# Half-projection pacing of tile 0's weight scalings, output-weight stores a step later, and the last pair's sums and output products woven in

## The chip, the cores and the metric

One core of one Trainium2 chip runs the whole program as a single launch. The metric is device microseconds from start to end; the time before is the median of three runs, 2706.23 us (2701.7 to 2709.22). A core has five engines that run side by side, each through its own list of instructions in order: TensorE (PE, matmuls and transposes), VectorE (DVE), ScalarE (ACT), GpSimd (POOL) and SyncE (SP, which here issues every DMA). They wait for each other through semaphores alone.

## The reference, cut to what matters

A trunk of two layers over 2048 frames of 1024 channels in float32: a gated MLP mixer, then attention in chunks of 64 frames, where each chunk sees itself and the 8 chunks before it. The change touches the second layer only.

```python
def chunk_attention_mixer(h, k_pad, v_pad, w_qz, rel_bias, w_out):
    q, z = jnp.split(h @ w_qz, 2, axis=-1)
    ...
        sc = jnp.einsum('bqhd,bkhd->bhqk', qc, kc).astype(jnp.float32) + bias
        sc = jnp.where(valid[None, None, None, :], sc, NEG_INF)
        p = jax.nn.softmax(sc, axis=-1).astype(vc.dtype)
        return jnp.einsum('bhqk,bkhd->bqhd', p, vc)
    ...
    return (o * jax.nn.silu(z)) @ w_out

    h = rms_norm(x, b_norm_g[i])
    x = x + chunk_attention_mixer(h, k_pad, v_pad, ...)
    return rms_norm(x, final_norm_g)
```

K and V come once from the residual stream behind the first layer, normalised with their own gain.

## The kernel before

**Numbers.** Every float32 factor is split in two: a part rounded for TensorE (`wh`, `hi`, `Sho`; a cast on ACT) and what is left (`wl`, `lo`, `Slo`; a subtraction on DVE). `mm3` (L113 to L115) multiplies with three matmuls: high by high, high by low, low by high.

**Stages.** The first layer takes about half of the time and then V follows for all tiles. From about 1530 us the attention runs over 4 tiles `t` of 512 frames, and in each over 8 pairs `p` of heads: tile 0 to about 1730, tile 1 to 2050, tile 2 to 2330, tile 3 to 2649 us. A pair has 8 steps `u` (two heads, four blocks of 128 queries). A step scores a block two steps ahead (`s`, L1324), takes its row maximum on DVE and its exp on ACT, scales it by the sum on POOL (`pr`, L1343), and transposes a block (`flip`: `tp`, L1359), which is then cast to `pt` on ACT and completed on DVE (L1363, L1364). There is one PSUM buffer for `tp`, so the next transpose waits for DVE's part of the last. At the step's end of each head `pv` (L1384) multiplies `pt` with V; `ot` (ACT), `og` (DVE) and a gate close it.

**What fills TensorE between the steps.** A generator (`ahead`, L1593) yields single groups of matmuls, and the main loop (L1627) takes an even share at each half step. In it are the projections of the next pair (`one`, L1234: 8 groups of three for each of Q, K and the gate), and the output product of the tile before (`outs[t - 1]`). That product is a Strassen scheme (`strassen`, L260): 7 products `PHS` of 2 halves with 12 matmuls each, named `bo_<product>_<half>`, in 4 generator steps. Its right sides are weights (`wh_bo`, `wl_bo`) from DRAM, which live in 8 buffers, enough for two products; its left sides are sums of attention outputs, split into `Sho` and `Slo`.

**The weights of the projections.** For each pair and each of three matrices `weights` (L213) loads 128 x 1024 numbers. In tile 0 POOL multiplies them by the norm's gain (`scaled`, L194) and they are stored to `wk`; ACT casts (L209) and DVE subtracts (L210). Later tiles load the scaled ones from `wk` (L218).

**The weights of the output product** are summed once, by `o_sums` (L298), during the first four pairs of tile 1: four blocks `wo` are loaded (L306), POOL forms sums, and each of seven products is cast (`so_<product>h`, L313), completed (`so_..l`) and stored (`ows`, L316; one in `owf`, L311). The `so` tiles share four buffers.

**The last pair.** Behind tile 3 no attention is left, so its own output product runs alone. `last_open` (L1449) loads tile 3's attention outputs of pairs 0 to 5 ahead of the last pair and forms the left sums (`s3`, then `s1`, `s2`, `s4`, all on POOL; written as A_hl from A_hh and A_hl in the profile). Pairs 6 and 7 are written into the left sides by DVE (`last_og`, L1474), with the rest of the sums behind each. During the last pair `ahead` gives 12 steps of tile 2's product; the whole of `outs[3]` comes behind it.

**What sets the order.** Tile's list scheduler puts each engine's instructions in order at build time. Two helpers bend it with dependencies that exist for the scheduler alone and make no semaphore: `on_beat` (L174) ties an instruction behind the last transposes of the step, `paced_by_pj` (L183) behind the latest entry of `pace`, which `one` appends to at the first group of each projection (L1241).

Of the kernel before, what the change touches and what calls it, by code (L numbers as in the profile page):

```python
# [22 lines left out]
NT = S // T  # L23
# [10 lines left out]
def trunk_kernel(  # L34
# [148 lines left out]
    def paced_by_pj(ins):  # L183
        if pace:
            tc.add_manual_dep(
                ins.ins, pace[-1],
                mybir.DependencyInfo(mybir.DependencyClass.NoSync, mybir.DependencyReason.DATA),
                reason="order",
            )
# [23 lines left out]
    def weights(t, p, c):  # L213
        name = f"b{t}_{p}_{c}"
        raw = raw_w(t, f"raw_{name}")
        w = w_tile(f"wh_{name}"), w_tile(f"wl_{name}")
        if t:
            nc.sync.dma_start(raw[:], wk3[p][c][:])  # L218
        else:
            nc.sync.dma_start(raw[:], w_kqz[p, :, c, :])  # L220
            paced_by_pj(scaled(raw, (bg if c else kg)[:, :, :]))
            nc.sync.dma_start(wk3[p][c][:], raw[:])
        hi = split_in(raw, *w)
        if t:
            paced_by_pj(hi)
        return w
# [72 lines left out]
    def o_sums(u, place, s_place):  # L299
# [8 lines left out]

        def keep(ph, src):
            if ph == 5:  # L310
                nc.sync.dma_start(owf[q][:, cs], src)  # L311
# [3 lines left out]
            for n, y_ in enumerate((hi, lo)):  # L315
                nc.sync.dma_start(ows[ph, q][:, n, cs], y_[:].bitcast(F32))  # L316
# [17 lines left out]
        ]  # L334
# [876 lines left out]
    with ExitStack() as bctx:  # L1211
# [22 lines left out]
        def one(t, p, c):  # L1234
            wh, wl = weights(t, p, c)
            acc = pmm.tile([P, T], F32, tag="mm", name=f"pj{t}_{p}_{c}")
            for k in range(KD):
# [3 lines left out]
                if k == 0:  # L1241
                    pace.append(ins.ins.name)
# [206 lines left out]
        def last_open():  # L1449
# [9 lines left out]
            for cs in (slice(0, 512), slice(512, 1024)):  # L1459
                tg(la["s3"][:, cs], la["00"][:, cs], la["10"][:, cs], op=sub)  # L1460
            last_sums(slice(0, 512))

        def last_sums(cs):
            x_ = {n: a[:, cs] for n, a in la.items()}
            tg(x_["s1"], x_["10"], x_["11"], op=add)
            tg(x_["s2"], x_["11"], x_["s3"], op=sub)
            tg(x_["s4"], x_["01"], x_["s2"], op=sub)

        def last_og(p, og32, z):
# [7 lines left out]
            last_sums(slice(k * 256, k * 256 + 256))  # L1477
# [120 lines left out]
        def ahead(t, p):  # L1598
# [8 lines left out]
            else:  # L1607
# [6 lines left out]
                if t:  # L1614
                    yield from some(outs[t - 1], 8)

        def steps_of(t, p):
            n = (32 if p == 0 else 24) if p + 1 < NPAIR else (16 if t + 1 < NT else 0)
            return n + SHARE[t][p]
# [10 lines left out]
        for t in range(NT):  # L1630
            for p in range(NPAIR):
                gen = ahead(t, p) if t + p else first
                total = steps_of(t, p) - (0 if t + p else 8)
                if t + 1 == NT and p + 1 == NPAIR:
                    last_open()
                per = 11 if p + 1 == NPAIR and t + 1 < NT else 16
                todo = []
                if t == 1 and p < 4:
# [89 lines left out]
```

## Time and profile before

| what | value |
|---|---|
| runs | 2701.7, 2706.23, 2709.22 us; median 2706.23 |
| profiled execution | 2705.63 us, of which the span is 2703.8 us |
| mean granted clock of TensorE | 0.992 |
| PE busy | 2625.2 us in 12960 records |
| DVE, ACT, POOL busy | 1887.0, 1295.5, 887.1 us |
| DMA | 735.53 MB, mean 272 GB/s |

The span is the stretch from the first to the last instruction of one profiled execution; the rest of that execution's time lies around it. Rows of the timeline give the start in us from the span's begin, the duration in us, engine, line, operation, what is written from what, and the count; in brackets stands how long the engine was idle before and what ended that. A row of the windows gives a stretch, its length, the busy time of PE, PEld (weight loads), DVE, ACT and POOL with counts, the granted clock, the DMA share and GB/s. A matmul's row overlaps the next, since PE is pipelined: the distance of two starts tells its cost.

### The profile page before, as it was taken

The numbers are of one execution on the slowest core, as the hardware profiler recorded it, in microseconds if no ns is written. First come the engines' busy times: TensorE is split into PE (matmuls) and PEld (weight loads), VectorE is DVE, ScalarE is ACT, GpSimd is POOL, SyncE is SP. The second block draws the span as 40 slices with busy tenths as digits, with TensorE's granted clock in tenths as the row PEclk, the third lists the DMA queues.
The fourth block names the chain that finished last, engine by engine and source line by source line (L and its number), as shares of the span: only waits on it lengthen the run. The fifth ranks groups of instructions, "written<-read, shape, count | busy, mean of one in ns | idle before, by whom it ended". The sixth has DMA issues, their size and how long they took to land.

```text
span 2703.8 us, 38109 instructions
## 1 busy us (share of the span) xinstructions
PE 2625.2 (97%) x12960; PEld 2188.7 (81%) x12960; DVE 1887.0 (70%) x2937; ACT 1295.5 (48%) x2296; POOL 887.1 (33%) x874
## 2 busy tenths in 40 slices
PE   8999999999999999999989999999998999999997
PEld 7888888888888888888868777777887888888875
DVE  5655676666677668757677766788767667866676
ACT  5422242443434435333365456666555555655553
POOL 3511335142251414115043344333332223313243
PEclk9999999999999999999999999999999999999999
DMA  7898999989988879858666677788889667766567
GB/s 297 313 328 329 343 363 324 333 318 342 329 314 280 309 257 333 294 203 274 247 241 210 221 250 228 223 275 293 281 264 292 203 217 241 254 204 197 183 228 245
DMA packets 274771, 735.53 MB, mean 272 GB/s; under 512 B 29585, under 2 KB 61329, under 8 KB 274577
## 3 DMA queue, kind: packets, MB, share of 16 engines
q1 hardware_dynamic: 274576, 733.09, 78.5%
q8 instruction: 104, 1.70, 0.3%
q14 instruction: 91, 0.74, 0.1%
HBM read 540.56 MB, written 181.93 MB: 267 GB/s over the span
## 4 chain that ended last, share of the span: by engine, by line
PE 77%; DVE 8%; DMA 7%; issue 3%; POOL 2%; ACT 2%; SPq 1%; DVEq 0%; POOLq 0%; ACTq 0%
PE P L115 11%; PE P L114 11%; PE P L113 11%; PE pj L113 5%; PE pj L115 5%; PE pj L114 5%; PE pv L1384 4%; PE s L1324 4%; PE tp L1359 3%; PE Po L115 2%; PE Po L113 2%; PE Po L114 2%; PE vp L115 2%; PE vp L114 2%; PE vp L113 2%
## 5 line engine op out<-in xcount | busy, mean ns | idle before, releaser
L113 PE MATMUL P<-T,S 128*128 128x512 f32 x1248 | 496.0, 397 | 2.1 <-ACT S L386 2.1
L115 PE MATMUL P<-T,S 128*128 128x512 f32 x1248 | 490.3, 393 | 0.0
L114 PE MATMUL P<-T,S 128*128 128x512 f32 x1248 | 489.1, 392 | 1.1 <-DVE T L389 1.1
L1343 POOL TENSOR_SCALAR pr<-pr,sl 128x640 f32<-128x640 f32 (+4 forms) x256 | 196.3, 768 | 543.3 <-DVE sl L1342 486.8
L113 PE MATMUL pj<-hh_b,wh_b 128*128 128x512 f32 x768 | 319.6, 416 | 1.8 <-ACT hh_b L168 1.0
L115 PE MATMUL pj<-hh_b,wl_b 128*128 128x512 f32 x768 | 304.7, 397 | 0.3 <-DVE wl_b L210 0.2
L114 PE MATMUL pj<-hl_b,wh_b 128*128 128x512 f32 x768 | 303.3, 395 | 0.0
L1339 ACT ACTIVATE pr<-pr,nm 128x640 f32<-128x640 f32 (+4 forms) x256 | 195.4, 763 | 192.8 <-DVE nm L1332 184.7
L115 PEld LDWEIGHTS P<-T,S 128*128 128x128 f32 x1248 | 235.3, 189 | 50.3
L113 PEld LDWEIGHTS P<-T,S 128*128 128x128 f32 x1248 | 235.9, 189 | 47.4 <-ACT S L386 2.3
L114 PEld LDWEIGHTS P<-T,S 128*128 128x128 f32 x1248 | 235.7, 189 | 46.9 <-DVE T L389 1.3
L1364 DVE TENSOR_TENSOR pt<-tp,pt 128x640 fp32r<-128x640 f32 (+4 forms) x256 | 188.8, 738 | 55.4 <-ACT pt L1363 52.1
L1332 DVE CUSTOM_DVE_ANT_0 pr<-s,bias 128x640 f32<-128x640 f32 (+4 forms) x256 | 188.1, 735 | 30.5 <-PE s L1324 26.2
L1363 ACT CAST pt<-tp 128x640 fp32r<-128x640 f32 (+4 forms) x256 | 159.1, 622 | 61.4 <-PE tp L1359 57.6
L1359 PE MATMUL tp<-ident,pr 128*128 128x128 f32 x1120 | 168.4, 276 | 19.0 <-DVE pt L1364 13.1
L1359 PEld LDWEIGHTS tp<-ident,pr 128*128 128x128 f32 x1120 | 130.8, 141 | 54.9 <-issue 22.3
L115 PEld LDWEIGHTS pj<-hh_b,wl_b 128*128 128x128 f32 x768 | 144.9, 189 | 32.9 <-DVE wl_b L210 1.7
L1384 PEld LDWEIGHTS pv<-pt,V 128*128 128x128 f32 x896 | 144.3, 191 | 31.5 <-DVE pt L1364 11.6
L1384 PE MATMUL pv<-pt,V 128*128 128x256 f32 (+3 forms) x896 | 158.5, 323 | 9.2 <-DVE pt L1364 6.4
L113 PEld LDWEIGHTS pj<-hh_b,wh_b 128*128 128x128 f32 x768 | 145.9, 190 | 19.9 <-ACT wh_b L209 1.6
L114 PEld LDWEIGHTS pj<-hl_b,wh_b 128*128 128x128 f32 x768 | 145.9, 190 | 17.5 <-issue 0.2
L210 DVE TENSOR_TENSOR wl_b<-raw_b,wh_b 128x1024 fp32r<-128x1024 f32 x96 | 126.9, 1322 | 42.3 <-ACT wh_b L209 41.0
(284 smaller groups left out, 5715.6 us busy)
## 6 DMA issues: line engine op xcount, KB each, us to landing
S<-hsd SPq DMA_DIRECT2D x288, 512.0 KB, 5.4
rw<-in_w_a SPq DMA_DIRECT2D x108, 512.0 KB, 6.3
A<-ytd SPq DMA_DIRECT2D x72, 512.0 KB, 5.7
raw_b<-wk SPq DMA_DIRECT2D x72, 512.0 KB, 4.7
hsd<-S SPq DMA_DIRECT2D x56, 512.0 KB, 4.4
V<-vhd SPq DMA_DIRECT2D x56, 512.0 KB, 5.6
wh_bo<-ows SPq DMA_DIRECT2D x50, 512.0 KB, 4.2
wl_bo<-ows SPq DMA_DIRECT2D x50, 512.0 KB, 5.8
```

The costliest lines, as they stand in the source:

```text
L113: first = mm(ps, lh, rh, start=first, stop=False)
L114: mm(ps, lh, rl, start=False, stop=False)
L115: mm(ps, ll, rh, start=False, stop=last)
L210: tv(wl[:], raw[:], wh[:].bitcast(F32), op=sub)
L1324: mm(ps[:, sg, :w], q[:, qb * P : (qb + 1) * P], kx[:, koff + sg * w : koff + (sg + 1) * w], start=i == 0, stop=i == 1,)
L1332: nc.vector.tensor_tensor_reduce(out=pr[:, c0:].rearrange("p (a b) -> p a b", a=nseg), in0=ps[:, :nseg, :w], in1=bias[:, c0:].rearrange("p ...
L1339: nc.scalar.activation(pr[:, c0:], pr[:, c0:], AF.Exp, scale=-1.0, bias=nm[:], accum_out=sl[:])
L1343: nc.gpsimd.tensor_scalar(pr[:, c0:], pr[:, c0:], sl[:], 1.0, op0=ALU.mult, op1=ALU.mult)
L1359: ins = tpose(tp[:, b, :], pr[:, b * P : (b + 1) * P], ident[:])
L1363: nc.scalar.copy(oh, tp[:, b0:5, :].rearrange("p a b -> p (a b)"))
L1364: nc.vector.tensor_tensor(pt[:, 2560 + o + b0 * P : 2560 + o + 640], tp[:, b0:5, :].rearrange("p a b -> p (a b)"), oh.bitcast(F32), op=ALU ...
L1384: mm(po[:, q0 * P : q1 * P], vtl[t, p][:, i, hs], rhs, start=(i == blocks[0] and j == 0), stop=(i == 7 and j == 1),)
```

## The change

Three edits of order and place; the same arithmetic is done.

1. `pace` also gets the fifth group of each projection (`k in (0, 4)`), so its entries lie half a projection apart. `paced_by_pj` goes back two entries by default, which is the same anchor as before; tile 0's scalings go back three.
2. In `o_sums` the stores of a product are kept in `pend` and issued at the next product, tied to that step's transposes; an eighth step issues the last.
3. `last_open` returns steps: `s3`, then `s1`, `s2`, `s4` of the first 512 columns one at a time, then all of columns 512 to 768. `last_og` of pair 6 forms no sums any more. `ahead` gives 13 steps of `outs[3]` in the last pair, which are products 1_0, 1_1, 7_0 and a quarter of 7_1: 39 matmuls.

```diff
--- before.py
+++ after.py
@@ -180,10 +180,10 @@
             )
         return ins
 
-    def paced_by_pj(ins):
+    def paced_by_pj(ins, back=2):
         if pace:
             tc.add_manual_dep(
-                ins.ins, pace[-1],
+                ins.ins, pace[-min(back, len(pace))],
                 mybir.DependencyInfo(mybir.DependencyClass.NoSync, mybir.DependencyReason.DATA),
                 reason="order",
             )
@@ -218,7 +218,7 @@
             nc.sync.dma_start(raw[:], wk3[p][c][:])
         else:
             nc.sync.dma_start(raw[:], w_kqz[p, :, c, :])
-            paced_by_pj(scaled(raw, (bg if c else kg)[:, :, :]))
+            paced_by_pj(scaled(raw, (bg if c else kg)[:, :, :]), 3)
             nc.sync.dma_start(wk3[p][c][:], raw[:])
         hi = split_in(raw, *w)
         if t:
@@ -306,14 +306,21 @@
             paced_by_pj(nc.sync.dma_start(w[rc][:], wb_out[rc[0], rc[1], q][:, cs]))
         b11, b12, b21, b22 = (w[k][:] for k in ((0, 0), (0, 1), (1, 0), (1, 1)))
 
+        pend = []
+
+        def stores():
+            while pend:
+                on_beat(nc.sync.dma_start(*pend.pop(0)))
+
         def keep(ph, src):
+            stores()
             if ph == 5:
-                nc.sync.dma_start(owf[q][:, cs], src)
+                pend.append((owf[q][:, cs], src))
             hi, lo = (s_place(f"so{u}_{ph}{x_}") for x_ in "hl")
             on_beat(nc.scalar.copy(hi[:], src))
             tv(lo[:], src, hi[:].bitcast(F32), op=sub)
             for n, y_ in enumerate((hi, lo)):
-                nc.sync.dma_start(ows[ph, q][:, n, cs], y_[:].bitcast(F32))
+                pend.append((ows[ph, q][:, n, cs], y_[:].bitcast(F32)))
 
         def first():
             keep(1, b11)
@@ -331,7 +338,7 @@
         return [first, second, third] + [
             lambda ph=ph, o=o: keep(ph, o)
             for ph, o in ((5, b11), (7, b12), (6, b22), (4, b21))
-        ]
+        ] + [stores]
 
     with ExitStack() as actx:
         ca = actx.enter_context(tc.tile_pool(name="ca", bufs=1))
@@ -1238,7 +1245,7 @@
                 hh, hl = xT[t][k]
                 sl = slice(k * P, (k + 1) * P)
                 ins = mm3(acc[:], wh[:, sl], wl[:, sl], hh, hl, k == 0, k == KD - 1)
-                if k == 0:
+                if k in (0, 4):
                     pace.append(ins.ins.name)
                 if k < KD - 1:
                     yield None
@@ -1456,15 +1463,25 @@
                         la[f"{r}{c}"][:, : k * 256],
                         ogd[NT - 1][:, r, 4 * c : 4 * c + k].rearrange("p k j s -> p (k j s)"),
                     )
-            for cs in (slice(0, 512), slice(512, 1024)):
-                tg(la["s3"][:, cs], la["00"][:, cs], la["10"][:, cs], op=sub)
-            last_sums(slice(0, 512))
+
+            def third():
+                for cs in (slice(0, 512), slice(512, 1024)):
+                    on_beat(tg(la["s3"][:, cs], la["00"][:, cs], la["10"][:, cs], op=sub))
+
+            def all_of(cs):
+                for f_ in last_sums(cs):
+                    f_()
+
+            return [third] + last_sums(slice(0, 512)) + [lambda: all_of(slice(512, 768))]
 
         def last_sums(cs):
             x_ = {n: a[:, cs] for n, a in la.items()}
-            tg(x_["s1"], x_["10"], x_["11"], op=add)
-            tg(x_["s2"], x_["11"], x_["s3"], op=sub)
-            tg(x_["s4"], x_["01"], x_["s2"], op=sub)
+            return [
+                lambda a=a, b=b, c=c, op=op: on_beat(tg(x_[a], x_[b], x_[c], op=op))
+                for a, b, c, op in (
+                    ("s1", "10", "11", add), ("s2", "11", "s3", sub), ("s4", "01", "s2", sub)
+                )
+            ]
 
         def last_og(p, og32, z):
             k = p - 4
@@ -1474,7 +1491,9 @@
                 nc.vector.scalar_tensor_tensor(
                     v4(la[f"{r}1"])[:, k], o4[:, r], 0.5, z4[:, r], op0=ALU.mult, op1=ALU.mult
                 )
-            last_sums(slice(k * 256, k * 256 + 256))
+            if p == 7:
+                for f_ in last_sums(slice(768, 1024)):
+                    f_()
 
         def last_left(ph, jp):
             n = {1: "00", 7: "s3", 2: "01", 6: "s2", 5: "s1", 4: "11", 3: "s4"}[ph]
@@ -1613,9 +1632,13 @@
                     values(t + 1, 0)
                 if t:
                     yield from some(outs[t - 1], 8)
+                if t + 1 == NT:
+                    yield from some(outs[t], 13)
 
         def steps_of(t, p):
             n = (32 if p == 0 else 24) if p + 1 < NPAIR else (16 if t + 1 < NT else 0)
+            if t + 1 == NT and p + 1 == NPAIR:
+                n = 13
             return n + SHARE[t][p]
 
         load_bias(0, 0)
@@ -1631,10 +1654,10 @@
             for p in range(NPAIR):
                 gen = ahead(t, p) if t + p else first
                 total = steps_of(t, p) - (0 if t + p else 8)
-                if t + 1 == NT and p + 1 == NPAIR:
-                    last_open()
                 per = 11 if p + 1 == NPAIR and t + 1 < NT else 16
                 todo = []
+                if t + 1 == NT and p + 1 == NPAIR:
+                    todo = last_open()
                 if t == 1 and p < 4:
                     todo = o_sums(p, lambda n: half_tile("C", n, 4), lambda n: half_tile(
                         "S", n, 4, F32R
```

How instructions move, at three places. The first is POOL between pairs 2 and 3 of tile 0 (`pr_4_2` is head 4, block 2; `raw_b_3_2` the weight of pair 3, matrix 2). Before:

```order
L1343 TENSOR_SCALAR pr_4_2_14266<-pr_4_2_14266,sl_4_2_14268 128x384
L1343 TENSOR_SCALAR pr_4_3_14315<-pr_4_3_14315,sl_4_3_14317 128x512
L1343 TENSOR_SCALAR pr_5_0_14339<-pr_5_0_14339,sl_5_0_14341 128x128
L194 TENSOR_TENSOR raw_b_3_2_14477<-raw_b_3_2_14477,bg 128x1024
L1305 MEMSET bias_6_14382 64x64
L1306 MEMSET bias_6_14382 64x64
L1343 TENSOR_SCALAR pr_5_1_14389<-pr_5_1_14389,sl_5_1_14391 128x256
L1343 TENSOR_SCALAR pr_5_2_14415<-pr_5_2_14415,sl_5_2_14417 128x384
```

Now:

```order
L1350 TENSOR_SCALAR pr_4_2_14266<-pr_4_2_14266,sl_4_2_14268 128x384
L194 TENSOR_TENSOR raw_b_3_2_14477<-raw_b_3_2_14477,bg 128x1024
L1350 TENSOR_SCALAR pr_4_3_14315<-pr_4_3_14315,sl_4_3_14317 128x512
L1312 MEMSET bias_6_14382 64x64
L1313 MEMSET bias_6_14382 64x64
L1350 TENSOR_SCALAR pr_5_0_14339<-pr_5_0_14339,sl_5_0_14341 128x128
L1350 TENSOR_SCALAR pr_5_1_14389<-pr_5_1_14389,sl_5_1_14391 128x256
L194 TENSOR_TENSOR raw_b_4_1_14560<-raw_b_4_1_14560,bg 128x1024
```

The scaling of `raw_b_3_2` stood behind three `pr` and stands behind one; that of `raw_b_4_1`, which stood behind `pr_5_2`, is ahead of it.

The second is SP in tile 1, at the weights for pair 4. Before:

```order
L316 DMA ows_1_113<-so_6h 128x512
L306 DMA wo_01_17171<-in_wb_out 128x512
L316 DMA ows_1_113<-so_6l 128x512
L1272 DMA khd_3_129<-K_3_1_17077 128x512
L316 DMA ows_1_109<-so_4h 128x512
L316 DMA ows_1_109<-so_4l 128x512
L306 DMA wo_11_17173<-in_wb_out 128x512
L306 DMA wo_10_17175<-in_wb_out 128x512
L218 DMA raw_b_4_0_17327<-wk_0_76 128x1024
```

Now:

```order
L313 DMA ows_1_105<-so_2h 128x512
L313 DMA ows_1_105<-so_2l 128x512
L218 DMA raw_b_4_1_17189<-wk_1_77 128x1024
L218 DMA raw_b_4_0_17325<-wk_0_76 128x1024
L313 DMA owf_117<-wo_00_16778 128x512
L313 DMA ows_1_111<-so_5h 128x512
L313 DMA ows_1_111<-so_5l 128x512
L313 DMA ows_1_115<-so_7h 128x512
```

The load of `raw_b_4_0` stood last, behind the stores of `so_6` and `so_4` and the loads of `wo`; now it is issued straight behind that of `raw_b_4_1`, ahead of the stores of `so_5`.

The third is PE in the last pair, at its last `pv` (`pv_15`, `tp_15_3` are head 15). Before:

```order
L1359 MATMUL tp_15_3_25409<-ident,pr_15_3_25359 128x128 x5
L1384 MATMUL pv_15_25424<-pt_15_25338,V_7_24944 128x512
L113 MATMUL bo_1_0_25471<-wh_bo_1_0_25459,Sho_0_25467 128x512
L114 MATMUL bo_1_0_25471<-wl_bo_1_0_25460,Sho_0_25467 128x512
L115 MATMUL bo_1_0_25471<-wh_bo_1_0_25459,Slo_0_25468 128x512
L113 MATMUL bo_1_0_25471<-wh_bo_1_0_25459,Sho_0_25467 128x512
L1384 MATMUL pv_15_25424<-pt_15_25338,V_7_24944 128x512 x3
L1384 MATMUL pv_15_25424<-pt_15_25338,V_7_24944 128x128 x2
L1384 MATMUL pv_15_25424<-pt_15_25338,V_7_24944 128x256 x2
L1384 MATMUL pv_15_25424<-pt_15_25338,V_7_24944 128x384 x4
L1384 MATMUL pv_15_25424<-pt_15_25338,V_7_24944 128x256 x2
L1384 MATMUL pv_15_25424<-pt_15_25338,V_7_24944 128x128 x2
```

Now, from the second row of that `pv` on:

```order
L1391 MATMUL pv_15_25523<-pt_15_25393,V_7_24944 128x512 x3
L1391 MATMUL pv_15_25523<-pt_15_25393,V_7_24944 128x128 x2
L1391 MATMUL pv_15_25523<-pt_15_25393,V_7_24944 128x256 x2
L1391 MATMUL pv_15_25523<-pt_15_25393,V_7_24944 128x384 x4
L1391 MATMUL pv_15_25523<-pt_15_25393,V_7_24944 128x256 x2
L1391 MATMUL pv_15_25523<-pt_15_25393,V_7_24944 128x128 x2
L114 MATMUL bo_7_1_25519<-wl_bo_7_1_25365,Sho_1_25493 128x512
L115 MATMUL bo_7_1_25519<-wh_bo_7_1_25364,Slo_1_25494 128x512
L113 MATMUL bo_7_1_25519<-wh_bo_7_1_25364,Sho_1_25493 128x512
L114 MATMUL bo_7_1_25519<-wl_bo_7_1_25365,Sho_1_25493 128x512
L115 MATMUL bo_7_1_25519<-wh_bo_7_1_25364,Slo_1_25494 128x512
L113 MATMUL bo_2_0_25567<-wh_bo_2_0_25482,Sho_0_25555 128x512
```

Before, the transposes of `tp_15_2` and `tp_15_3` were neighbours, four matmuls of product 1 stood inside the `pv`, and 44 of products 1 and 7 followed it. Now those stand between the transposes, five are left behind the `pv`, and then product 2 begins. Earlier in the same pair the first matmul of product 3 (`bo_3_0`) has moved too: it stood behind `tp_14_2`, ahead of the scores `s_15_1`; now it stands behind `tp_14_1`, ahead of the scores `s_15_0`, and `bo_3_1` is woven into it.

## The prediction

> **What bounds the kernel now.** The page comes first: its span and the busy share of each engine.
>
> ```profile
> span 2703.8 us, 38109 instructions
> PE 2625.2 (97%) x12960; PEld 2188.7 (81%) x12960; DVE 1887.0 (70%) x2937; ACT 1295.5 (48%) x2296; POOL 887.1 (33%) x874
> ```
>
> TensorE is busy for 97%, and the diff neither adds nor removes a matmul. So the change can only move the 3% in which PE waits, and the stretches in which it runs at a lower granted clock. Where these lie is told by the busy time by window (columns: stretch, length, PE, PEld, DVE, ACT, POOL, clock, DMA share, GB/s).
>
> ```profile
> 1600.00:1700.00 100.00, 96.19 (x481) 76.65 (x479) 67.07 (x167) 59.15 (x131) 40.57 (x57) 1.00 0.69 216
> 1800.00:1900.00 100.00, 94.63 (x516) 78.79 (x516) 82.98 (x150) 68.71 (x125) 38.62 (x47) 0.98 0.89 293
> 2600.00:2640.00 40.00, 33.60 (x179) 27.37 (x178) 28.23 (x57) 21.10 (x43) 22.89 (x25) 0.96 0.74 261
> 2640.00:2704.00 64.00, 47.52 (x194) 36.04 (x193) 41.88 (x61) 23.30 (x43) 21.35 (x18) 0.91 0.70 237
> ```
>
> The rows are the three stages that the diff touches, and their idle PE is the room of each part: about 4 us in 100 in tile 0 (part 1), 5 in 100 in tile 1 (part 2), 6.4 in 40 and 16.5 in 64 at the end (part 3).
>
> **Part 1, the scalings of tile 0.** Nothing is added; 24 POOL multiplies move. One pair, from the timeline:
>
> ```profile
> 1610.02 0.69 POOL L1343 TENSOR_SCALAR pr<-pr,sl 128x512 f32<-128x512 f32 x1 [4.71 <-DVE sl L1342]
> 1611.33 1.90 POOL L194 TENSOR_TENSOR raw_b<-raw_b,bg 128x1024 f32<-128x1024 f32 x1
> 1613.27 1.05 ACT L209 CAST wh_b<-raw_b 128x1024 fp32r<-128x1024 f32 x1 [1.15 <-POOL raw_b L194]
> 1614.32 0.39 PE L114 MATMUL pj<-hl_b,wh_b 128*128 128x512 f32 x1
> 1614.54 0.39 PE L115 MATMUL pj<-hh_b,wl_b 128*128 128x512 f32 x1
> 1615.59 0.58 ACT L1363 CAST pt<-tp 128x512 fp32r<-128x512 f32 x1
> 1615.60 0.39 PE L115 MATMUL pj<-hh_b,wl_b 128*128 128x512 f32 x1
> 1616.22 0.51 PE L1384 MATMUL pv<-pt,V 128*128 128x512 f32 x1 [0.23 <-ACT pt L1363]
> 1617.27 1.27 PE L1384 MATMUL pv<-pt,V 128*128 128x512 f32 x7 [0.54 <-DVE pt L1364]
> ```
>
> POOL idles 4.71 us, scales `pr`, and only then begins the weight. ACT waits 1.15 us for it; behind that cast stand the Q copy, an exp and the cast of `pt`, for which PE waits. The normal distance of two matmul starts is 0.22 to 0.23 us (1614.32 to 1614.54). From 1615.60 to 1616.22 it is 0.62, from there to 1617.27 it is 1.05: 0.39 + 0.82 = 1.21 us lost. How often, says the group of the ACT casts (who ended their idle time, us, times):
>
> ```profile
>   POOL raw_b L194: 8.2, 7
> ```
>
> 8.2 us in 7 waits, one per pair. With the scaling ahead of that `pr`, it fits into the 4.71 us of idle POOL and the cast is free 1.15 us sooner. Not all of the 1.21 goes, since the DVE subtraction behind the cast now falls next to other DVE work: I take 0.93 a pair, 7 x 0.93 = 6.5 us. Bounds: 0 if DVE takes the delay over, 1.21 x 7 = 8.5.
>
> The head of tile 0 has a wait of the same kind.
>
> ```profile
> 1544.17 0.14 POOL L1305 MEMSET bias<- 64x64 f32 x1 [21.90 <-DMA bias<-reld]
> 1550.54 0.39 PE L1324 MATMUL s<-K,Qh 128*128 128x256 f32 x1 [2.27 <-DVE nm L1332]
> ```
>
> A scaling stands behind memsets that wait 21.90 us for a load, its cast holds up ACT, and PE waits 2.27 us for the row maximum. The order now has that scaling ahead of the memsets. I take 2 us, bounds 0 to 4 (the wait, and as much again where PE is slow behind it).
>
> What speaks against part 1 is that a scaling now runs beside DVE work. The nearest row of two such, from tile 1:
>
> ```profile
> 1836.24 1.29 POOL L321 TENSOR_TENSOR wo<-wo,wo 128x512 f32<-128x512 f32 x1
> 1836.52 2.09 DVE L210 TENSOR_TENSOR wl_b<-raw_b,wh_b 128x1024 fp32r<-128x1024 f32 x1
> 1614.35 1.23 DVE L210 TENSOR_TENSOR wl_b<-raw_b,wh_b 128x1024 fp32r<-128x1024 f32 x1 [1.18 <-ACT wh_b L209]
> ```
>
> The same subtraction takes 2.09 us beside a POOL add and 1.23 without, 0.86 more. The Trainium skill has a rule for it ("SBUF — State Buffer", Who interferes with whom): a DVE instruction with two SBUF inputs and a GpSimd instruction that reads SBUF use one port pair, and whoever issues first holds the other for its whole length. The trace agrees, since 1836.24 + 1.29 + the usual 1.23 would end at 1838.76 and the row ends at 1838.61. By that rule alone part 1 would give most of its gain back. I keep it as a rival and not in the sum, because POOL is busy 41 us of 100 here and the old place of the scaling overlapped DVE too.
>
> **Part 2, stores of tile 1.** No transfer is added; the `ows` and `owf` stores of a product are issued with the next one. SP works in order, so weight loads that stood behind stores now stand ahead of them.
>
> ```profile
> 1868.35 1.05 ACT L209 CAST wh_b<-raw_b 128x1024 fp32r<-128x1024 f32 x1 [4.33 <-DMA raw_b<-wk]
> 1872.39 0.85 PE L1359 MATMUL tp<-ident,pr 128*128 128x128 f32 x5 [2.02 <-DVE pt L1364]
> 1872.00:1878.00 6.00, 5.61 (x25) 4.84 (x26) 4.87 (x11) 3.55 (x6) 4.31 (x3) 0.72 0.75 248
> 1817.47 0.62 ACT L313 CAST so_7h<-wo 128x512 fp32r<-128x512 f32 x1
> 1820.48 0.62 ACT L313 CAST so_6h<-wo 128x512 fp32r<-128x512 f32 x1
> DMA to landing us min/median/max: 2.1/3.0/5.2
> ```
>
> A late load holds ACT 4.33 us; PE pays 2.02, and then 6 x (1 - 0.72) = 1.7 for the clock. If the load of that weight (`raw_b_4_0`) comes sooner, 3.7 us go. Against it: the four `so` buffers are two products, and they are held a step longer. Casts follow each other after 3.01 us (1817.47 to 1820.48), and a store takes 3.0 us to land (the last row, of the stores in L316: issue to landing; the longest 5.2). So a cast would now wait for its predecessor's store by some tenths up to 1.5 us where SP is late, about once a pair, with ACT work behind it on which DVE and PE rest. I take 3.7 less 4 x 0.4 = 2 us of gain; bounds -5 (with a second weight of the same kind) and +6 (4 x 1.5, nothing gained).
>
> **Part 3, the last pair.** PE's waits from 2590 to the end (us, times, longest):
>
> ```profile
> PE tp L1359 <- POOL pr L1343: 3.8, 1, 3.8
> PE tp L1359 <- DVE pt L1364: 3.0, 2, 2.1
> PE bo L113 <- DMA wh_bo<-ows: 2.0, 3, 1.2
> PE bo L114 <- DMA wl_bo<-ows: 1.0, 2, 0.5
> PE pv L1384 <- ACT pt L1363: 0.8, 1, 0.8
> 2626.00:2632.00 6.00, 4.49 (x18) 4.03 (x19) 2.40 (x5) 2.10 (x4) 3.55 (x6) 0.72 0.28 113
> 2642.00:2648.00 6.00, 4.59 (x16) 3.61 (x17) 2.85 (x6) 0.69 (x1) 0.55 (x1) 0.72 0.96 255
> 2616.08 2.94 POOL L1460 TENSOR_TENSOR A_hl<-A_hh 128x512 f32<-128x512 f32 x2
> 2626.66 1.57 POOL L1343 TENSOR_SCALAR pr<-pr,sl 128x640 f32<-128x640 f32 x2
> ```
>
> From 2616.08 to 2626.66 POOL works through the sums, and the scaling of `pr` waits. That is 3.8 + 3.0 + 0.8 = 7.6 us of waits and 2 x 1.7 of clock, 11.0 in all. Spread one per step, a sum delays a `pr` by 1.5 at most, and 39 matmuls of the output product (39 x 0.23 = 9.0 us) now fill the gaps. What comes instead, by the new order and these rows:
>
> ```profile
> 2617.55 0.39 PE L113 MATMUL bo<-wh_bo,Sho 128*128 128x512 f32 x1
> 2621.32 0.47 PE L113 MATMUL bo<-wh_bo,Sho 128*128 128x512 f32 x1 [0.42 <-DMA wh_bo<-ows]
> 2649.48 0.58 ACT L1393 COPY ot<-pv 64x512 f32<-64x512 f32 x1 [5.38 <-PE pv L1384]
> 2650.82 0.76 DVE L1474 SCALAR_TENSOR_TENSOR A_hh<-og,Z 128x256 f32<-128x256 f32 x2
> ```
>
> The first matmul of product 3 (its weight landed just before 2621.32) is now reached at about 2617.6, where the row of 2617.55 stands: 3.7 us of waiting. And behind the last `pv` only five matmuls (5 x 0.23 = 1.2 us) are left before product 2, which needs `ot`, `og`, `A_hh` and a cast: 2649.48 to 2651.58, and some 0.6 for the cast, from a `pv` that ended at 2649.2. From 2649.2 to 2652.2 and 0.3 for the issue are 3.3 us of chain against 1.2 of cover: 2.1 us, once. Removed 11.0, new 3.7 + 2.1 = 5.8: 5.2 gained. The stretch after it has 2.0 + 1.0 us of waits on weights; the 9 us of work moved ahead let these loads start sooner against PE, and I count 2.3 of them. Together 7.5. Bounds: 11.0 + 3.0 = 14 gained if neither new wait comes; 2 lost if both do with a slow clock behind each (5.8 + 2 x 1.7 = 9.2, against the 7.6 of waits removed).
>
> The Trainium skill ("TensorE: Matmul & The Clock Gate", Part 1) has the clock fall after an idle window of about 3.4 us. By that page a wait of 2.1 us would leave the clock alone; the row at 1872.39 has a wait of 2.02 with a clock of 0.72 behind it, so the measurement decides and the bound stays.
>
> **The sum.** 6.5 + 2 + 2 + 7.5 = 18 us off the profiled execution's 2705.6 (span 2703.8 and 1.8 around it): 2687.6. That execution lies 0.6 below the median of 2706.2, so I predict 2688. All good bounds at once (8.5 + 4 + 5 + 14) give 2674, all bad ones (0, 0, +6, +2) 2714. Its own range is 2678 to 2698.
>
> **Rivals.**
>
> *The shared port takes tile 0's gain.* A scaling beside DVE costs up to 0.86 on a DVE that feeds PE: 7 x 0.86 = 6.0 of the 6.5, and the head's 2 as well. For it: the rows at 1836. Against: DVE is 67 busy in 100 in that stage. Time: 2688 + 8 = 2696.
>
> *The end is bound by its weights.* The interleaved products ask for four 512 KB weights a phase earlier, while stores of `y` stand ahead of them on SP. For it: 3.0 us of DMA waits stand there now, and a DMA share of 0.96 from 2642 to 2648. Against: a share of 0.28 from 2626 to 2632. Then part 3's 7.5 goes: 2695.5.
>
> *Everything goes through.* Neither new wait of part 3 comes: 2688 - 6 - 4 = 2678.
>
> *Slower: held buffers.* The four `so` buffers make ACT wait for a store at every product, not once a pair. There are 4 pairs x 7 = 28 casts; at 1.5 us each and PE paying 3.7 for 4.33 of ACT (0.86, the rows at 1868) it is 28 x 1.5 x 0.86 = 36, against a forecast without part 2's gain (2690): 2726. It decides from 1 us a cast (28 x 0.86 = 24, 2714). For it: 3.0 to land against 3.01 between casts. Against: ACT is 69 busy in 100, and most casts lie further apart.
>
> **How the numbers follow.** Forecast 0.55, port 0.12, weights 0.13, all through 0.10, held buffers 0.10. A measurement of this kernel can tell about 0.3%, 8 us, from no change: faster is below 2698, slower above 2714. Faster: 0.50 of the forecast, 0.10, and 0.15 of port and weights, 0.75. Slower: the held buffers and a little of the forecast's bad bounds, 0.11. Same: 0.14. For 8 in 10 the range reaches down to the case where all goes through and up past port and weights: 2676 to 2707.
>
> **What would show it.** Part 1: in tile 0 no ACT cast waits for POOL's L194 and the `pv` waits of 0.23 and 0.54 are gone; if subtractions of 1.23 grow to 2 us there, it is the port. Part 2: no wait of 4.33 on a weight in tile 1, and no cast of `so` that waits for a store. Part 3: no wait of PE for `pr` near 2627, matmuls of `bo` ahead of the last `pv`, one wait of about 3.7 at product 3's first weight and one of about 2.1 behind the last `pv`. It is wrong if PE's waits on weights grow over 3 us after the last pair, or if ACT waits over 1 us at most of the 28 casts.

## The result, and the profile after

The changed kernel takes 2691.4 us (median of 6 runs, 2685.92 to 2698.01), the kernel before on the same chip 2705.57 (6 runs, 2701.46 to 2712.34): a ratio of 0.9947, interval 0.9925 to 0.9969, or 14 us less. In a second comparison the same two stood at 2692.28 and 2704.61, ratio 0.9962 (0.9949 to 0.9975), 10 us less. (Gains in us are worked out from the ratio here and below; by the medians this second one is 12.) Forecast were 18 us less. So the direction holds and the size is under the forecast; where the gain sits differs from the forecast more than the sum does.

The profiled execution after the change is the slowest of its six (2698.01), so its span of 2696.2 is no measure of the gain, but its parts are. Busy time by window (columns as before), for the first two stages of the attention and the last pair with what follows:

```profile
span 2696.2 us, 38071 instructions
1600.00:1700.00 100.00, 98.67 (x511) 82.39 (x510) 72.38 (x178) 63.61 (x141) 42.41 (x63) 1.00 0.76 237
1800.00:1900.00 100.00, 96.61 (x530) 79.65 (x529) 83.73 (x149) 68.61 (x122) 34.59 (x44) 1.00 0.90 295
2600.00:2697.00 97.00, 72.97 (x322) 57.15 (x321) 64.33 (x106) 39.79 (x78) 39.76 (x38) 0.89 0.68 242
```

Idle PE in the window of tile 0 fell from 3.8 to 1.3 us, in that of tile 1 from 5.4 to 3.4. The end did not improve: 24.0 of 97 us idle, at a clock of 0.89; before, the prediction's two rows for it had 22.9 of 104, at 0.96 and 0.91.

**Tile 0.** Two rows of PE after the change, and the same two a pair later (in brackets the idle time before and what ended it):

```profile
1615.21 1.38 PE L1391 MATMUL pv<-pt,V 128*128 128x512 f32 x8
1619.58 0.41 PE L1366 MATMUL tp<-ident,pr 128*128 128x128 f32 x2 [0.33 <-DVE pt L1371]
...
1639.58 1.38 PE L1391 MATMUL pv<-pt,V 128*128 128x512 f32 x8
1643.94 0.41 PE L1366 MATMUL tp<-ident,pr 128*128 128x128 f32 x2 [0.33 <-DVE pt L1371]
```

The `pv` runs through as one row of eight, without the two waits of 0.23 and 0.54 that cut it. The period is 1643.94 - 1619.58 = 24.36 us; before it was 25.77 (the row of 1616.22 and its successor at 1641.99). The POOL and ACT rows of the same pair show why:

```profile
1605.02 1.90 POOL L194 TENSOR_TENSOR raw_b<-raw_b,bg 128x1024 f32<-128x1024 f32 x1
1608.83 1.03 ACT L209 CAST wh_b<-raw_b 128x1024 fp32r<-128x1024 f32 x1
1609.29 0.69 POOL L1350 TENSOR_SCALAR pr<-pr,sl 128x512 f32<-128x512 f32 x1 [2.38 <-DVE sl L1349]
```

The scaling lies in POOL's idle time ahead of that `pr`, and the cast starts 1.9 us after it ended, without a wait.

**The end.** PE's waits from 2590 us on (us in all, times, longest):

```profile
PE bo L115 <- DVE Slo L296: 7.1, 3, 3.7
PE bo L113 <- DMA wh_bo<-ows: 5.1, 2, 3.5
PE bo L113 <- ACT Sho L295: 1.4, 1, 1.4
PE pv L1391 <- DVE rr_f L127: 0.6, 1, 0.6
PE bo L114 <- DMA wl_bo<-ows: 0.5, 2, 0.3
```

The waits for `pr` and `pt` (3.8, 3.0, 0.8) are gone, as forecast, and others of the same size stand in their place: 14.7 us in this list, against 13.6 in the whole list before. The row of `Slo` grew most; the prediction's list doesn't have it. Before it read:

```profile
PE bo L115 <- DVE Slo L296: 2.2, 2, 1.6
```

### The profile page after: what moved, and what is told of

Read it like the earlier page. It is cut to its first block, busy times and chain, and to the rows that moved or that the text cites. A ratio compares the mean times of both kernels' runs of the same rounds, so it can differ in the third digit from the quotient of the medians.

```text
span 2696.2 us, 38071 instructions
## 1 busy us (share of the span) xinstructions
PE 2627.2 (97%) x12960; PEld 2197.9 (82%) x12960; DVE 1892.0 (70%) x2937; ACT 1296.6 (48%) x2296; POOL 888.2 (33%) x874
## 4 chain that ended last, share of the span: by engine, by line
PE 81%; DVE 7%; DMA 6%; issue 2%; ACT 2%; POOL 2%; SPq 1%; DVEq 0%; POOLq 0%; ACTq 0%
PE P L115 11%; PE P L114 11%; PE P L113 11%; PE pj L115 5%; PE pj L113 5%; PE pj L114 5%; PE pv L1391 4%; PE Po L113 4%; PE Po L114 4%; PE Po L115 4%; PE s L1331 4%; PE tp L1366 3%; PE vp L115 1%; PE vp L113 1%; PE vp L114 1%
## 5 line engine op out<-in xcount | busy, mean ns | idle before, releaser
L113 PEld LDWEIGHTS P<-T,S 128*128 128x128 f32 x1248 | 236.2, 189 | 46.9 <-ACT S L393 2.3
L1371 DVE TENSOR_TENSOR pt<-tp,pt 128x640 fp32r<-128x640 f32 (+4 forms) x256 | 188.7, 737 | 49.2 <-ACT pt L1370 46.2
L210 DVE TENSOR_TENSOR wl_b<-raw_b,wh_b 128x1024 fp32r<-128x1024 f32 x96 | 125.8, 1311 | 26.9 <-ACT wh_b L209 25.3
```

What stands on the lines that cost most here:

```text
L113: first = mm(ps, lh, rh, start=first, stop=False)
L210: tv(wl[:], raw[:], wh[:].bitcast(F32), op=sub)
L1371: nc.vector.tensor_tensor(pt[:, 2560 + o + b0 * P : 2560 + o + 640], tp[:, b0:5, :].rearrange("p a b -> p (a b)"), oh.bitcast(F32), op=ALU ...
```

## The experiments

All variants are compared with the kernel before on the same chip; its median lies between 2704.6 and 2706.7 us in the four comparisons. The program ahead of the last pair is the same in every variant with parts 1 and 2 (save the one that moves steps to earlier pairs), on all five engines' lists. Yet its length differs between executions: in the two profiles of the whole change the last projection matmul starts at 2594.24 and at 2586.96 us.

```profile
2594.24 0.40 PE L115 MATMUL pj<-hh_b,wl_b 128*128 128x512 f32 x1
```

```profile
2586.96 0.40 PE L115 MATMUL pj<-hh_b,wl_b 128*128 128x512 f32 x1
```

So a difference of some microseconds between two totals can't be put down to part 3. From here on part 3 is also judged by a local length: from the start of that last projection matmul to the end of the span, with the last `pv` row's end as the mark between.

| variant | median us | ratio (interval) | last projection to `pv`'s end | to the span's end | both |
|---|---|---|---|---|---|
| before | - | 1 | 46.3 | 54.4 | 100.7 |
| part 1 alone | 2696.4 | 0.9972 (0.9962 to 0.9983) | 48.3 | 55.0 | 103.2 |
| part 2 alone | 2703.0 | 0.9991 (0.9982 to 1.0000) | 48.6 | 55.2 | 103.8 |
| part 3 alone | 2703.7 | 0.9996 (0.9986 to 1.0006) | 50.0 | 52.5 | 102.5 |
| parts 1 and 2 | 2694.9 | 0.9966 (0.9953 to 0.9979) | 46.9 | 55.1 | 102.0 |
| 1, 2, sums alone | 2688.5 | 0.9933 (0.9921 to 0.9945) | 41.7 | 54.7 | 96.4 |
| 1, 2, matmuls alone | 2688.0 | 0.9936 (0.9923 to 0.9949) | 50.0 | 51.2 | 101.1 |
| whole change | 2691.4 | 0.9947 (0.9925 to 0.9969) | 50.8 | 51.1 | 102.0 |
| whole change again | 2692.3 | 0.9962 (0.9949 to 0.9975) | 49.8 | 52.4 | 102.1 |
| whole, Slo first | 2687.9 | 0.9930 (0.9915 to 0.9945) | 50.1 | 46.2 | 96.3 |
| sums, Slo first | 2690.3 | 0.9948 (0.9934 to 0.9961) | 42.4 | 55.7 | 98.1 |
| sums, Slo first, 4 steps | 2693.1 | 0.9953 (0.9939 to 0.9968) | 49.1 | 54.3 | 103.4 |
| whole, 10 steps | 2696.0 | 0.9963 (0.9950 to 0.9976) | 52.2 | 50.3 | 102.4 |
| whole, six steps earlier | 2693.0 | 0.9955 (0.9943 to 0.9967) | 49.5 | 50.5 | 100.0 |

(The last variant has 18 matmuls, 4.1 us, fewer on this stretch.) Each local length is of one execution and is worked out from three numbers of its profile: for the sums alone the rows are these (start, duration), and the span is 2686.3, so 2628.25 + 3.36 - 2589.93 = 41.7 and 2686.3 - 2631.61 = 54.7.

```profile
2589.93 0.40 PE L115 MATMUL pj<-hh_b,wl_b 128*128 128x512 f32 x1
2628.25 3.36 PE L1391 MATMUL pv<-pt,V 128*128 128x512 f32 x15
```

The four kernels without any of part 3 (before, parts 1 and 2 alone and together) have the same lists on this stretch and show 100.7 to 103.8, the three executions with all of it 102.0 to 102.5. So the local length too spreads by 3 us, and smaller differences are not read. Most of that spread goes with the granted clock: up to the last `pv` it is 0.93 before and with parts 1 and 2, and 0.86 with part 1 or part 2 alone, the two longest.

### The parts alone

Part 1 alone:

```diff
-    def paced_by_pj(ins):
+    def paced_by_pj(ins, back=2):
-                ins.ins, pace[-1],
+                ins.ins, pace[-min(back, len(pace))],
-            paced_by_pj(scaled(raw, (bg if c else kg)[:, :, :]))
+            paced_by_pj(scaled(raw, (bg if c else kg)[:, :, :]), 3)
-                if k == 0:
+                if k in (0, 4):
                     pace.append(ins.ins.name)
```

> Part 1 alone (scalings of tile 0 half a projection earlier). Theory of the prediction: 8.5 us faster than before (6.5 in the steady pairs, 2 at the head), ratio 0.9969. Rival (shared port takes it): 0 to 2 us faster. From the profile after the change, where the pair's period fell from 25.77 to 24.36 us seven times over, up to 10 us could go, ratio 0.9963.

Measured: 2696.36 (7 runs) against 2704.61 (18 runs), ratio 0.9972 (0.9962 to 0.9983): 7.6 us, between 4.6 and 10.3. That is the forecast's size; the 0 to 2 us of the rival (the shared port takes it) lie outside.

Part 2 alone (the `pend` list and `stores` of the diff, nothing else):

> Part 2 alone (stores a step later). Forecast: 2 us faster than before, ratio 0.9993; by the profile the ACT wait of 4.33 on the weight of pair 4 is gone. Rival (held buffers): 2 us or more slower, with ACT casts of so waiting for stores.

Measured: 2702.96 (12 runs) against 2706.01 (17 runs), ratio 0.9991 (0.9982 to 1.0000): 2.4 us, between 0 and 4.9, so by itself it is not clear of no gain. The held buffers don't make it slower. Both of the forecast's effects are seen in ACT's waits of tile 1 (1730 to 1900 us), in the profile before (first) and after the whole change (second):

```profile
ACT wh_b L209 <- DMA raw_b<-wk: 7.3, 4, 4.3
```

```profile
ACT wh_b L209 <- DMA raw_b<-wk: 4.4, 2, 3.0
ACT so_5h L320 <- DMA ows<-so_3h: 2.4, 3, 1.1
```

The waits on weights fell from 7.3 to 4.4 us and the one of 4.3 is gone. New are three waits of a cast for the store two products back, 2.4 us together, and in the same list one of 1.3 of `Sho` for a store of `so_4`: the forecast had four of 0.4. In the profile of part 2 alone the weights stand at 4.4 us too, and the cast of `so_5` waits once, 1.7 us.

Part 3 alone, and parts 1 and 2 without it:

> Part 3 alone (last pair's sums one per step, 39 matmuls of the output product inside). Theory: 7.5 us faster than before, ratio 0.9972. Rival: new waits (the first weight of product 3, Slo behind the y scales) eat all of it, within 2 us of before.

> Parts 1 and 2 without part 3. Theory of the prediction: part 3 is worth 7.5 us, so this is 10.5 us faster than before (ratio 0.9961) and 7 slower than the whole change. Rival: in the profiled execution after the change the last pair and the tail show as much lost time as before, so part 3 is worth nothing and this equals the whole change, 14 us faster (ratio 0.9948).

Part 3 alone: 2703.72 (11 runs), ratio 0.9996 (0.9986 to 1.0006). Without it: 2694.93 (6 runs), ratio 0.9966 (0.9953 to 0.9979). Part 3 alone can't be told from no change; 7.5 us lie outside its interval (a gain of at most 3.8). Beside the other two it is worth 10.3 - 9.2 = 1 us in the same comparison, with overlapping intervals. Locally nothing of it can be told: 102.0 to 102.5 with it, 100.7 to 103.8 without.

The whole change a second time:

> The whole change once more, for a second profile and a time beside the parts on the same chip: 2691 us, ratio 0.995 if the parts are additive as the forecast has it (8.5 + 2 + 7.5 = 18 would be 0.9933). Theory on the spread (2686 to 2698): the waits in the tail (Slo behind the row scales, 2.5 to 3.7 us each) differ from run to run, and this profile shows another tail than the first.

Measured as given above; the expected spread of the tail was wrong. Its waits are nearly the first profile's:

```profile
PE bo L115 <- DVE Slo L296: 6.9, 3, 3.4
PE bo L113 <- ACT pt L1370: 3.9, 1, 3.9
PE bo L113 <- ACT Sho L295: 1.4, 1, 1.4
PE bo L113 <- DMA wh_bo<-ows: 1.4, 1, 1.4
```

(The second row is the first weight of product 3 again. The profile puts the wait down to an ACT cast that ended 0.1 us ahead of the matmul; but the matmul reads nothing of that cast, and its weight, issued at 2597.24, landed at 2605.29, just ahead of the matmul at 2605.43.) The 7 us between the two profiles lie ahead of the last pair.

### Part 3 taken apart

The sums one per step, without the matmuls (beside parts 1 and 2):

```diff
                 if t:
                     yield from some(outs[t - 1], 8)
-                if t + 1 == NT:
-                    yield from some(outs[t], 13)
...
             n = (32 if p == 0 else 24) if p + 1 < NPAIR else (16 if t + 1 < NT else 0)
-            if t + 1 == NT and p + 1 == NPAIR:
-                n = 13
```

> Parts 1 and 2, and of part 3 only the sums one per step; the 39 matmuls stay behind the last pair. Theory A (POOL's block of sums is what holds the last pair): the wait of 4.1 us for pr and the clock behind it go, so it is about 5 us faster than parts 1 and 2 alone (2690, ratio 0.995). Rival B (the last pair lacks matmuls, and its chain of transposes, casts and subtractions sets its length): the wait only changes its name, within 2 us of parts 1 and 2 alone (2695, ratio 0.9966).

Measured: 2688.54 (6 runs), ratio 0.9933. That is 6.4 us under parts 1 and 2 by the medians (two comparisons on different chips, whose intervals don't overlap), and by the local length 96.4 against 100.7 to 103.8: 4.3 to 7.4 us. Theory A holds. Only POOL's list differs between these two kernels. PE's waits from 2580 us on, first two rows with parts 1 and 2, then rows with the sums:

```profile
PE tp L1366 <- POOL pr L1350: 4.1, 1, 4.1
PE tp L1366 <- DVE pt L1371: 3.0, 2, 2.1
```

```profile
PE tp L1366 <- DVE pt L1371: 3.0, 2, 2.1
PE bo L115 <- DVE Slo L296: 2.3, 3, 1.6
PE bo L113 <- DMA wh_bo<-ows: 1.2, 1, 1.2
PE pv L1391 <- ACT pt L1370: 0.8, 1, 0.8
PE tp L1366 <- POOL pr L1350: 0.2, 1, 0.2
```

The wait for `pr` fell from 4.1 to 0.2. Those for `pt` stayed as they were: POOL's block was not their cause.

The matmuls without the sums (`some(outs[t], 13)` kept, `last_open` as before the change):

> Parts 1 and 2, and of part 3 only the 39 matmuls inside the last pair; the sums stay in one block ahead of it. Theory (the sums gain 6 and the matmuls give 4 to 8 back): 3 to 8 us slower than parts 1 and 2 alone, 2698 to 2703, ratio 0.998. Rival (the two need each other: only with matmuls between them do the waits go): within 2 us of parts 1 and 2 alone (0.9966), or faster.

Measured: 2688.04 (5 runs), ratio 0.9936. By the total the rival wins; by the local length of 101.1, within 100.7 to 103.8, nothing was gained or lost. Its profile reaches the last projection matmul at 2583.67, 10 us ahead of parts 1 and 2 (2594.11), with the same instructions up to there; so its good total is not shown to come from part 3. What goes with it is the granted clock: ahead of that matmul TensorE runs 20.5 us at half clock here and 37.5 with parts 1 and 2, a difference of 17.0 that is worth up to 8.5 us; and the mean clock of its five executions has a median of 0.993, that of the six with parts 1 and 2 of 0.990. Why the clock was higher stays open.

By the local lengths the sums alone are better than the matmuls alone and than both together. On top of the sums the matmuls cost 102.0 - 96.4 = 5.6 us: they lengthen the pair by 8.1 to 9.1 us, about their whole 39 x 0.23 = 9.0, and shorten what follows by only 2.3 to 3.6. The rows by window say why; each time first up to the end of the last `pv`, then from there to the last matmul. Parts 1 and 2, with the sums, whole change:

```profile
2594.11:2640.97 46.86, 36.96 (x190) 30.14 (x189) 31.25 (x62) 21.50 (x44) 22.31 (x25) 0.93 0.77 256
2640.97:2687.44 46.47, 41.31 (x165) 31.05 (x163) 32.72 (x43) 20.30 (x36) 19.07 (x15) 0.96 0.68 243
2589.93:2631.61 41.68, 35.68 (x190) 28.79 (x189) 31.17 (x62) 21.49 (x44) 22.45 (x25) 0.96 0.88 290
2631.61:2677.58 45.97, 41.22 (x164) 30.68 (x163) 32.79 (x43) 20.29 (x36) 18.87 (x15) 0.96 0.69 243
2594.24:2645.07 50.83, 44.78 (x229) 37.15 (x228) 33.84 (x66) 26.24 (x51) 22.76 (x25) 0.93 0.78 276
2645.07:2687.78 42.71, 33.95 (x125) 24.80 (x124) 31.35 (x40) 15.53 (x29) 18.28 (x15) 0.92 0.65 232
```

The sums took PE's idle time in the pair from 9.9 us to 6.0. With the matmuls it is 6.0 again, so they filled nothing on balance: waits for weights came for those that they covered. Behind the `pv`, where they are missing, idle time rose from 4.8 to 8.8 us.

### What the matmuls meet

Ten steps in place of 13:

```diff
-                    yield from some(outs[t], 13)
+                    yield from some(outs[t], 10)
...
-                n = 13
+                n = 10
```

> The whole change with 10 instead of 13 steps of the own product in the last pair, so that 18 matmuls (4.1 us) instead of 5 are left behind the last pv. Theory: the waits behind it (1.4 for Sho and 2.5 for Slo) shrink to under 1, and the pair loses little in return: 1 to 3 us faster than the whole change. Rival: the y scale ahead of Slo on DVE still ends the wait, within 1 us.

Measured: 2695.97 (6 runs), ratio 0.9963, locally 102.4. No gain: the longest wait for `Slo` is down to 2.1, but a wait of 2.5 for a low weight (`wl_bo`) has come up, and the stretch up to the last `pv` is 52.2.

Six steps of tile 2's product moved to the earlier pairs:

```diff
-            (0,) * 8, ..., (2, 7, 7, 7, 7, 7, 7, 12)
+            (0,) * 8, ..., (2, 8, 8, 8, 8, 8, 8, 6)
```

> The whole change with six steps of tile 2's product moved from the last pair to the six before it, so that product 3 comes later against its weights and 19 instead of 25 steps lie in the last pair. Theory: the wait of 3.5 us at product 3's first weight goes, 2 to 4 us faster than the whole change. Rival: product 5 frees its buffers earlier too and the last pair then lacks matmuls, no gain or 2 us slower.

Measured: 2692.96 (6 runs), ratio 0.9955: no difference from the whole change can be told. The wait on the first weight is gone, and in its place PE waits 4.8 us for `Sho` and, from 2570 us on, 5.1 in all for `pt` (3.2 of it in the last pair):

```profile
PE bo L113 <- ACT Sho L295: 5.2, 2, 4.8
PE tp L1366 <- DVE pt L1371: 5.1, 3, 3.2
```

This fits a pair and a step into product 2 that have a length of their own (transpose, cast, subtraction; then `ot`, `og`, `A_hh`, `Sho`), where matmuls that are taken from one place are missing at the other.

The scalings of finished rows put behind the subtractions that PE waits for (with `los`, the names of the `Slo` instructions, and a dependency for the scheduler alone):

```diff
+    def behind_lo(ins):
+        tc.add_manual_dep(
+            ins.ins, los[-1],
+            mybir.DependencyInfo(mybir.DependencyClass.NoSync, mybir.DependencyReason.DATA),
+            reason="order",
+        )
+        return ins
...
-                    if last:
+                    if last and (r, c, jp) == (0, 1, 1):
                         finish(b)
...
-                        if not last:
+                        if los_on:
+                            behind_lo(ins)
+                        elif not last:
                             on_beat(ins)
...
-                    if u and finals:
+                    if u and finals and (u < 6 or p + 1 < NPAIR or t + 1 < NT):
...
-        run(outs[NT - 1])
+        los_on.append(1)
+        for n, _ in enumerate(outs[NT - 1]):
+            if finals and (n in (5, 9, 13) or n >= 37):
+                finals.pop(0)()
```

> The whole change with four scalings of finished rows on DVE put behind the Slo subtractions of products 2 and 3, for which PE waits (y_0 behind both of product 2, row 1 behind the second of product 3). Theory: PE's waits on Slo in the tail fall from 6.9 us to 2 or less, 4 to 5 us faster than the whole change (2687). Rival: the Slo waits hide a wait on weights or ACT that comes next, 0 to 2 us faster.

Measured: 2687.88 (6 runs), ratio 0.9930 (0.9915 to 0.9945), locally 96.3 against 102.0 and 102.1: 5.7 us. The rows of the whole change name the cause on DVE:

```profile
2648.69 1.88 DVE L1549 SCALAR_TENSOR_TENSOR y<-y,rr_f,gf 128x512 f32<-128x512 f32 x2 [1.43 <-DMA y<-x2d]
2650.49 1.28 DVE L296 TENSOR_TENSOR Slo<-A_hh,Sho 128x512 fp32r<-128x512 f32 x2
2678.81 2.41 DVE L1549 SCALAR_TENSOR_TENSOR row<-row,rr_f,gf 128x512 f32<-128x512 f32 x2 [0.66 <-POOL rr_f L128]
2681.74 0.68 DVE L296 TENSOR_TENSOR Slo<-A_hl,Sho 128x512 fp32r<-128x512 f32 x1
2682.47 0.50 PE L115 MATMUL bo<-wh_bo,Slo 128*128 128x512 f32 x1 [3.74 <-DVE Slo L296]
```

A scaling of `y` waits 1.43 us for its load with `Slo` behind it, and one of `row` waits 0.66 for POOL; PE stands still for both. With `Slo` first this is left, and behind the last `pv` the row by window is the third one:

```profile
PE bo L113 <- DMA wh_bo<-ows: 5.6, 2, 4.2
PE bo L115 <- DVE Slo L305: 2.3, 2, 1.4
2634.81:2671.99 37.18, 31.23 (x125) 22.38 (x124) 31.76 (x40) 15.26 (x28) 19.51 (x15) 1.00 0.73 253
```

Set beside the whole change's row (42.71 long, clock 0.92), PE idles 5.9 us in place of 8.8, and the same 125 matmuls keep it busy for 31.2 in place of 34.0. So of these 5.5 us about half are waits of PE, and the other half goes with the clock, which stays full.

The same reordering of row 1 with the sums alone, and with 4 steps of matmuls:

> Parts 1 and 2, the sums one per step, no own matmuls in the last pair, and the scaling of finished row 1 put behind the last Slo subtraction on DVE. Theory: the last Slo waits (0.7 and 1.9 us with the sums alone) go, 2 to 3 us faster than the sums alone, ratio 0.992. Rival: the last rows then close later, no gain.

> As the one with sums and Slo first, with 4 steps (12 matmuls, 2.8 us) of the own product in the last pair. Theory: waits of 3.0 for the subtraction of pt and 0.8 for its cast remain at the end of the pair and take 12 matmuls without asking for weights early: 1 to 3 us faster. Rival: as with 13 steps, product 3 comes ahead of its weights, 1 to 3 us slower.

Measured: 2690.32 (6 runs), ratio 0.9948, locally 98.1; and 2693.1 (6 runs), ratio 0.9953, locally 103.4. Neither beats the sums alone (96.4). The first shows no gain, as its rival has it: the longest wait for `Slo` fell from 1.6 to 0.6, but the stretch behind `pv` grew by 1.0, and the time from the last matmul to the end from 8.7 to 9.9. In the second product 3 comes ahead of its weight again: the longest wait for one is 2.5.

## Why the prediction was right, and where not

The time lies in the range, and the direction holds. That 14 of 18 us came is in part luck of the runs, since the second comparison has 10. By the prediction's terms:

- **Part 1**, 6.5 + 2 = 8.5 us: measured 7.6 alone. The mechanism is as forecast: ACT's waits for the scaling fell from 8.2 us to 3.6 (the list of tile 0: 9 waits, the longest 0.7), so its sign "no ACT cast waits for POOL's L194" came in the main and not in full. The split was off: if all seven pairs fell like the one shown, the steady pairs gave 7 x 1.41 = 9.9, above the bound of 8.5. The two gaps of 1.21 went whole; where the other 0.2 a pair came from was not followed. At the head PE's waits shrank by little: 2.3 for `nm` and 1.2 for `Qh` became 2.9 for `Qh`. From a matmul at 1531 us to one at 1563 the whole change is 1.0 us shorter, part 1 alone 2.9, so the 2 us of the head are neither shown nor refuted.
- **The shared port** cost little: the subtraction L210 between 1550 and 1720 us has a mean of 1237 ns before and 1288 after (first and second row below), 20 of them: 1 us of DVE in all, where the rival had 0.86 each. The runs don't tell whether the rule cited from the Trainium skill ("SBUF — State Buffer", Who interferes with whom) is at work in so small a rise.

```profile
L210 DVE TENSOR_TENSOR wl_b<-raw_b,wh_b 128x1024 fp32r<-128x1024 f32 x20 | 24.7, 1237 | 13.7 <-ACT wh_b L209 13.5
```

```profile
L210 DVE TENSOR_TENSOR wl_b<-raw_b,wh_b 128x1024 fp32r<-128x1024 f32 x20 | 25.8, 1288 | 10.3 <-ACT wh_b L209 9.8
```

- **Part 2**, 2 us: measured 2.4 (0 to 4.9). The wait of 4.33 is gone, and the clock of 1800 to 1900 us rose from 0.98 to 1.00. The price for it was higher than the forecast's 4 x 0.4, and its sign "no cast of `so` that waits for a store" did not come; it contradicted that price.
- **Part 3**, 7.5 us: mis-sized. It measured 1.1 alone (0.9996: 3.8 gained to 1.6 lost), and by the local length no gain can be told. The 11.0 us were put down to POOL's block of sums whole; without that block 4.3 to 7.4 went, and the waits of 3.0 and 0.8 for `pt` stayed. Of the steps, "3.7 us of waiting" at product 3's first weight was right (3.5, and 3.9 in the second profile). The step "2.1 us, once" behind the last `pv` (1.9 by its own rows, since that `pv` ended at 2649.4) was too small: 1.4 for `Sho` and then 2.5 for `Slo` (7.1 in three waits with the two later ones), because the cover was reckoned against `Sho` alone and the scaling of `y` that stands ahead of `Slo` on DVE was left out. Not foreseen at all was the 3.7 near the end, a wait that was 1.6 before. And the term "39 x 0.23 = 9.0 us now fill the gaps" treated matmuls as cover for waits that have their own cause: the waits for weights moved with them, and idle time in the pair is 6.0 us with and without them. The bound of that term (2 lost) did hold the result.

The rival "the end is bound by its weights" gave 2695.5 and was right in that part 3's gain went, and in one place (two weights, 5.1 us, both ahead of the last `pv`). The larger share of the waits (7.1 us) was DVE's order: `Slo` first takes 2.8 us of idle time behind the `pv` away, and the clock is full there. The total stayed inside because 10.5 of the 18 forecast microseconds lie in parts 1 and 2, and those came.

Two versions are better than the whole change by the local length and by the median: the sums alone (96.4; 2688.5) and `Slo` first (96.3; 2687.9). By the medians that is 3 to 4 us; both intervals overlap that of the whole change's first comparison, though not that of its second, and the chips differ. The 5.7 us of the local length are outside its spread, but each of the two rests on one profile. Between these two no difference can be told. Not tried: the weights of product 3 loaded ahead of the last pair's `A_hh`, together with `Slo` first.

## What to carry to other kernels

When work is moved into a stretch with idle time, ask what each idle stretch waits for: matmuls fill a wait only if their own operands (weights, casts, subtractions) are there at that moment, and the place they leave has lost its cover. Take a change of several edits apart one by one; here one half of an edit was worth 4 to 7 us, and with the other half beside it nothing of that was left. Where totals of the same program spread by several us, measure from a mark inside the program that all variants share, and look at the granted clock of the stretch before a difference is put down to the edit.

## What the runs showed of the hardware

**The clock.** In all 14 traces TensorE's granted clock is either full or half, and a stretch at half clock lasts 3.41 us or twice that (the last one of each trace aside). Three neighbouring stretches of 3.41 us from the first profile of the whole change:

```profile
2345.08:2348.49 3.41, 0.99 (x6) 0.57 (x5) 3.35 (x6) 0.48 (x1) 0.29 (x2) 1.00 0.83 305
2348.49:2351.90 3.41, 3.41 (x13) 2.91 (x12) 2.75 (x6) 1.82 (x5) 0.80 (x1) 0.50 0.28 80
2351.90:2355.31 3.41, 3.41 (x21) 3.09 (x20) 2.17 (x6) 2.77 (x7) 0.92 (x1) 1.00 0.35 112
```

In the first PE is idle for 2.42 us, in one wait for a row maximum; the second runs at half clock, which costs 1.7 us where PE is busy throughout; the third is at full clock again. Each trace can be cut in such stretches, from one of its changes of clock on. Then all 93 stretches at full clock with more than 1.93 us of idle PE were followed by half clock, none of 7818 with less than 1.6 was, and the 34 between went either way. So a wait well under 3.41 us is enough, short waits that fall in one stretch add up, and the same waits count or don't count by where the cuts lie. This is how a wait of 2 us comes to cost nearly 4, as in the prediction's row of 1872.39 (2.02 and 1.7).

**The spread.** The same program on the same inputs reached the same matmul at 2594.24 and at 2586.96 us in two executions, with every engine's list alike: 7 us of spread in the stretch that no edit of part 3 touches, as large as the effects looked for. Medians of five to seven runs did not remove it between variants (the matmuls alone). Much of it goes with the clock: ahead of that matmul 47.8 us ran at half clock in the first execution and 30.7 in the second, a difference worth up to 8.5 us. And of the six executions of the first comparison the longest (2698.0 us) has a mean clock of 0.987, the two shortest (2685.9 and 2687.0) 0.994. Waits lower the clock and a low clock moves the waits, and the runs don't separate the two: why one execution has more such stretches than another was not found.
